# One decoder layer on one core: the moving operand of the feature-major products is read from its last column to its first

## The chip, the cores and the metric

One core of a Trainium2 chip (trn2) runs the whole program. The metric is the device time of one execution in microseconds (us). The profile shows one execution; its span runs from the first to the last instruction of the core.

## What is computed

One hybrid decoder layer for 256 tokens of width 2048, in float32:

```python
proj = x @ w_in                                  # 16 heads of 128: q, k, v
a_out = diff_attention(q_d, k_d, v_d, ...)       # 8 heads, two sub-heads of 64, softmax(1) - lam * softmax(2)
b_out = moba_attention(q_m, k_m, v_m, ...)       # 8 heads, causal (256 tokens are one block)
h = LayerNorm(alpha * x + concat(a_out, b_out) @ w_out)
u = h @ w_up; g, val = u[..., :5632], u[..., 5632:]
gc = conv_b + sum(conv_w[j] * shifted(g, j))     # causal convolution over 3 tokens
out = LayerNorm(alpha * h + (silu(gc) * val) @ w_down)
```

## The kernel before

**Products from halves.** Every float32 operand of the large products is split into a high part rounded to a shorter mantissa and a low part (the remainder), both of the type fp32r. A product is then hi·hi + hi·lo + lo·hi. ACT makes the high part of a weight tile (L138, `split`), DVE the low part (L139); both go two stream steps ahead of the product.

**The stream.** Weights come as 1 MB tiles in one fixed order, `stream`: four groups of four v tiles followed by the q and k tiles of four heads; 16 tiles of the output projection; 43 further pairs of gate and value tiles of the feed-forward part (kinds g and u; the first pair is computed another way, in `mm_first`); 44 tiles of the down projection (kind d). For each tile the loop calls `begin(i)` (splits for later tiles, the next load, work due at this step), the product with `middle(i)` in its middle, and `done(i)`. What is due at a step was registered with `at(step, fn, ...)`. So the order on every engine is written out by hand.

**Feature-major products** (`mm_feature`) are those whose output has features on the partitions and tokens on the columns: q and k of each head (32 tiles) and the gate and value tiles (86). The weights are the stationary operand and the tokens move: `x2` and `h2` are tiles [128, 16, 2, 256] in SBUF, for each of 16 contraction blocks the high parts of the 256 tokens followed by their low parts. For each block one product of 512 columns multiplies the high weights with both, which fills a whole PSUM bank [hi·hi | hi·lo], and a second of 256 columns adds lo·hi to the half that holds hi·hi. Afterwards `added` (L219, L220) takes the bank apart: ACT copies one half to SBUF, DVE adds the other half to it. It is called by `qk_out` for q and k, one step after the product and before the rotation (`rope`, L268 to L271), the scores (two steps after the k tile) and the softmax; by `up_out` for the gate and value tiles, followed by `gated` (L443 to L446) and `act_out` (L450). q and k use banks 0 and 1 in turn; gate and value tiles go around all eight.

Token-major products (v, the output projection, the down projection), the transposes, the scores and the products with probabilities don't use `mm_feature` or `added`. The scores' operands and the probabilities are plain float32, not fp32r. In the profile `bank<-h,hi` is a product that writes a bank, moves the tile h (`h2`) and holds hi (the high weights); `bank<-x,lo` moves `x2` against the low weights. All products share L206.

Of the kernel before, what the change touches and what calls it, by code (L numbers as in the profile page):

```python
# [13 lines left out]
AF = mybir.ActivationFunctionType  # L14
ALU = mybir.AluOpType
# [3 lines left out]
S = 256  # L19
# [5 lines left out]
KT = D // P  # L25
# [25 lines left out]
def hymba_layer(ctx: ExitStack, tc: tile.TileContext, a: dict):  # L51
    nc = tc.nc
    PE, DVE, ACT, POOL, SP = nc.tensor, nc.vector, nc.scalar, nc.gpsimd, nc.sync
# [88 lines left out]
    def weights(i, x, w):  # L142

        hi, lo = parts[i, x // 1024]
        return hi[:, x % 1024:x % 1024 + w], lo[:, x % 1024:x % 1024 + w]
# [59 lines left out]
    def mm(out, lhsT, rhs, start, stop):  # L205
        PE.matmul(out, lhsT, rhs, start=start, stop=stop)  # L206

    def mm_feature(dst, i, t2):

        for k in range(KT):  # L210
            if k == KT // 2:
                middle(i)
            wh, wl = weights(i, k * P, P)
            mm(dst, wh, t2[:, k].rearrange("p j t -> p (j t)"), k == 0, False)
            mm(dst[:, 0:S], wl, t2[:, k, 0], False, k == KT - 1)

    def added(dst, src):

        ACT.activation(dst, src[:, S:2 * S], AF.Copy)  # L219
        DVE.tensor_tensor(dst, src[:, 0:S], dst, ALU.add)  # L220

    def mm_token(dst, i, x, ah, al, first, last):

# [30 lines left out]
    def qk_out(h, j):  # L254
        if j == 0:
            att[h] = work.tile([P, 2, S], F32, name="m1")
        added(att[h][:, j], bank[j])
# [166 lines left out]
    def summed(f, j):  # L424
        t = work.tile([P, S], F32, name="gu"[j] + "s", tag=f"e{j}", bufs=3)
        added(t, u_bank(f, j))
        return t
# [149 lines left out]
    def middle(i):  # L577

        urgent(i + 0.5)
        if i + 2 < NS and seven(i + 2):  # L580
            blocks_lo(i + 2, 0)
            blocks_sum(i + 2, 0)
            blocks_lo(i + 2, 1)
            act_sums_split(i + 2)
            blocks_hi(i + 2, 0)
            split(i + 3, 0)
            blocks_lo(i + 2, 2)
        elif i + 3 < NS and not seven(i + 3):
            split(i + 3, 0)
        pending(i + 0.5)  # L590
# [14 lines left out]
    def run_a(i):  # L605
        kind, h, kc, _ = stream[i]
        if kind == "v":
# [10 lines left out]
            return  # L618
        j = "qk".index(kind)
        mm_feature(bank[j], i, x2)  # L620
        done(i)
        if i < first_o - 1:
# [195 lines left out]
    for i in range(first_u + 2, first_d):  # L818
        begin(i)
        kind, f, _, _ = stream[i]  # L820
        j = "gu".index(kind)
        mm_feature(u_bank(f, j), i, h2)
        done(i)
        if i < first_d - 1:
            at(i + 1, up_out, f, j)
        else:
            up_out(f, j)
        if j == 1 and 3 <= f < 11:
            at(i + 1.5, h_piece, f - 3)
# [90 lines left out]
    for i in range(first_d, NS - PAIRED_END):  # L920
        begin(i)
        _, p, n, _ = stream[i]
# [167 lines left out]
```

## Time and profile before

| | before |
|---|---|
| median of 3 runs | 1138.34 us (1137.75 to 1139.84) |
| the profiled execution | 1139.33 us, of which the span 1137.5 us |
| PE (products) busy | 1124.0 us, 99% |
| PEld (weight loads) busy | 962.2 us, 85% |
| DVE busy | 810.0 us, 71% |
| ACT busy | 614.7 us, 54% |
| mean granted clock of TensorE | 0.997 of full speed |

PE's and PEld's records overlap, and so do the records of neighbouring products: the recorded length of a product includes the time until its last column has left the array, so the distance between the starts of neighbouring products, not their length, is what each costs. Idle time of an engine that isn't the bottleneck costs nothing.

### The profile page before, as it was taken

Reading aid. Unit: us, or ns where it says so; the run is one execution under the profiler, and the core shown is the slowest. Engines: PE = TensorE matmul, PEld = TensorE weight load, DVE = VectorE, ACT = ScalarE, POOL = GpSimd, SP = SyncE. Lnnn points to the kernel's source line nnn. Section 1 sums busy time; section 2 is a strip of 40 time slices with the busy share of each in tenths; the row PEclk is TensorE's granted clock in tenths of the full one; section 3 lists DMA queues with packets and bytes.
Section 4 is the critical chain, followed back from the end, with each engine's and each line's share of the span. In section 5 each row is a group of like instructions: output and inputs, shape, how many; then the busy total and the mean of one; then the engine's idle time right before and its main releaser. Section 6 shows DMA issues by size and latency. Waiting matters only on the chain.

```text
span 1137.5 us, 15607 instructions
## 1 busy us (share of the span) xinstructions
PE 1124.0 (99%) x5971; PEld 962.2 (85%) x5971; DVE 810.0 (71%) x1373; ACT 614.7 (54%) x1007; POOL 30.1 (3%) x38
## 2 busy tenths in 40 slices
PE   9999999999999999999999999999999999999996
PEld 6888888888888898888888888888888888888875
DVE  6895886857745777777566666656666788899885
ACT  6565564444443375545545454555545677667661
POOL 0000000000000000000000000000000000000004
PEclk9999999999999999999999999999999999999998
DMA  9755454545455546555555555555555678777951
GB/s 344 270 222 194 150 185 154 180 172 169 177 185 185 185 173 237 187 197 193 199 185 186 185 186 190 192 199 193 188 186 186 185 232 258 243 218 229 305 189 74
DMA packets 47323, 226.56 MB, mean 199 GB/s; under 512 B 4624, under 2 KB 6544, under 8 KB 27664
## 3 DMA queue, kind: packets, MB, share of 16 engines
q1 hardware_dynamic: 45664, 216.92, 53.8%
q0 software_dynamic: 1584, 8.65, 3.8%
q8 instruction: 46, 0.75, 0.3%
q14 instruction: 29, 0.24, 0.1%
HBM read 214.80 MB, written 2.10 MB: 191 GB/s over the span
## 4 chain that ended last, share of the span: by engine, by line
PE 97%; DMA 1%; DVE 1%; ACT 0%; issue 0%; POOL 0%; SPq 0%; ACTq 0%
PE bank L206 96%; DMA slot<-raw 1%; PE bank L329 0%; DMA raw<-in_w_v 0%; DVE z L977 0%; PE bank L705 0%; PE bank L376 0%; ACT hf L708 0%; ACT slot L516 0%; DVE h L720 0%; DVE st L400 0%; DVE z L397 0%; POOL rstd L408 0%; DVE z L1019 0%; DVE bank L1018 0%
## 5 line engine op out<-in xcount | busy, mean ns | idle before, releaser
L139 DVE TENSOR_TENSOR lo<-raw,hi 128x1024 fp32r<-128x1024 f32 (+1 forms) x372 | 440.6, 1199 | 212.6 <-ACT hi L138 212.4
L138 ACT ACTIVATE hi<-raw 128x1024 fp32r<-128x1024 f32 (+1 forms) x372 | 380.1, 1035 | 229.3 <-PE bank L206 199.6
L206 PE MATMUL bank<-h,hi 128*128 128x512 f32 x1376 | 477.2, 390 | 0.0
L206 PE MATMUL bank<-h,lo 128*128 128x256 f32 x1376 | 388.1, 282 | 0.0
L206 PEld LDWEIGHTS bank<-h,hi 128*128 128x128 f32 x1376 | 258.4, 188 | 53.9
L206 PEld LDWEIGHTS bank<-h,lo 128*128 128x128 f32 x1376 | 260.5, 189 | 0.0
L206 PE MATMUL bank<-x,hi 128*128 128x512 f32 x512 | 181.6, 396 | 0.0
L206 PE MATMUL bank<-x,lo 128*128 128x256 f32 x512 | 144.3, 282 | 0.0
L206 PEld LDWEIGHTS bank<-x,hi 128*128 128x128 f32 x512 | 96.1, 188 | 21.6 <-issue 1.3
L206 PEld LDWEIGHTS bank<-x,lo 128*128 128x128 f32 x512 | 96.9, 189 | 0.2
L206 PE MATMUL bank<-hi,x 128*128 128x512 f32 x256 | 86.6, 408 | 0.6 <-ACT hi L138 0.6
L206 PEld LDWEIGHTS bank<-hi,x 128*128 128x128 f32 x256 | 49.2, 192 | 13.2 <-ACT hi L138 1.5
L443 ACT ACTIVATE gc<-gs,vec 128x256 f32<-128x256 f32 x43 | 25.9, 602 | 58.6 <-DVE gs L220 58.6
L206 PE MATMUL bank<-lo,x 128*128 128x512 f32 x128 | 51.6, 403 | 0.0
L446 ACT ACTIVATE gc<-gc 128x256 f32<-128x256 f32 x44 | 18.4, 418 | 48.9 <-DVE gc L445 48.9
L206 PE MATMUL bank<-hi,mh 128*128 128x512 f32 x128 | 42.1, 400 | 0.0
L206 PE MATMUL bank<-lo,mh 128*128 128x512 f32 x128 | 41.6, 396 | 0.0
L206 PE MATMUL bank<-hi,ml 128*128 128x512 f32 x128 | 41.6, 395 | 0.0
L444 DVE SCALAR_TENSOR_TENSOR gc<-gs,vec,gc 128x255 f32<-128x255 f32 x43 | 20.8, 484 | 28.8 <-ACT gc L443 28.8
L206 PE MATMUL bank<-hi,ah 128*128 128x512 f32 (+1 forms) x126 | 40.3, 395 | 0.0
L206 PE MATMUL bank<-lo,ah 128*128 128x512 f32 (+1 forms) x126 | 39.7, 389 | 0.0
L206 PE MATMUL bank<-hi,al 128*128 128x512 f32 (+1 forms) x126 | 39.6, 389 | 0.0
(176 smaller groups left out, 1284.1 us busy)
## 6 DMA issues: line engine op xcount, KB each, us to landing
raw<-in_w_u SPq DMA_DIRECT2D x88, 1024.0 KB, 4.8
raw<-in_w_d SPq DMA_DIRECT2D x88, 512.0 KB, 6.0
raw<-in_w_qk SPq DMA_DIRECT2D x32, 1024.0 KB, 4.9
raw<-in_w_o SPq DMA_DIRECT2D x16, 1024.0 KB, 4.8
raw<-in_w_v SPq DMA_DIRECT2D x12, 1024.0 KB, 4.8
slot<-raw POOLq DMA_DIRECT2D x11, 768.0 KB, 9.0
raw<-in_w_v SPq DMA_DIRECT2D x8, 256.0 KB, 4.4
raw<-in_w_v SPq DMA_DIRECT2D x4, 512.0 KB, 7.2
```

What stands on the lines that cost most here:

```text
L138: ACT.activation(hi[:, s], t[:, x:y], AF.Copy)
L139: DVE.tensor_tensor(lo[:, s], t[:, x:y], hi[:, s].bitcast(F32), ALU.subtract)
L206: PE.matmul(out, lhsT, rhs, start=start, stop=stop)
L443: ACT.activation(gc, g, AF.Identity, bias=vec[:, C_CB + f:C_CB + f + 1], scale=w[2])
L444: DVE.scalar_tensor_tensor(gc[:, 1:], g[:, 0:S - 1], w[1], gc[:, 1:], op0=ALU.mult, op1=ALU.add)
L446: ACT.activation(gc, gc, AF.Silu)
```

## The change

In `mm_feature` both products read the tokens with a step of -1: column 0 of the bank gets the last low part, column 511 the first high part. hi·hi then lies backwards in columns 256 to 511, and lo·hi is added there, also from tokens read backwards. `added` reads both halves of the bank backwards, so that its output has the tokens in their old order. Nothing else differs: the same number of products, of the same sizes, on the same banks, at the same places of the order, with the weights as before; no transfer is changed.

```diff
             wh, wl = weights(i, k * P, P)
-            mm(dst, wh, t2[:, k].rearrange("p j t -> p (j t)"), k == 0, False)
-            mm(dst[:, 0:S], wl, t2[:, k, 0], False, k == KT - 1)
+            mm(dst, wh, t2[:, k].rearrange("p j t -> p (j t)")[:, ::-1], k == 0, False)
+            mm(dst[:, S:2 * S], wl, t2[:, k, 0, ::-1], False, k == KT - 1)
 
     def added(dst, src):
 
-        ACT.activation(dst, src[:, S:2 * S], AF.Copy)
-        DVE.tensor_tensor(dst, src[:, 0:S], dst, ALU.add)
+        ACT.activation(dst, src[:, 0:S][:, ::-1], AF.Copy)
+        DVE.tensor_tensor(dst, src[:, S:2 * S][:, ::-1], dst, ALU.add)
```

## Rows read from the trace of the kernel before

**Rows 1.** The page: busy time of each engine with its share of the span and its instructions, and the granted clock of TensorE in 40 equal slices of the span (tenths of full speed, 9 is 90% or more).

```profile
PE 1124.0 (99%) x5971; PEld 962.2 (85%) x5971; DVE 810.0 (71%) x1373; ACT 614.7 (54%) x1007; POOL 30.1 (3%) x38
PEclk9999999999999999999999999999999999999998
```

**Rows 2.** All waits of PE: who waited for whom, us in total, times, the longest.

```profile
PE bank L206 <- DVE idle L546: 1.2, 1, 1.2
PE bank L206 <- DVE h L720: 0.7, 1, 0.7
PE bank L206 <- ACT hi L138: 0.6, 1, 0.6
```

**Rows 3.** Groups of instructions by line, operands and shape, the four forms of the feature-major products: count, busy us, mean ns of one, idle time before.

```profile
L206 PE MATMUL bank<-h,hi 128*128 128x512 f32 x1376 | 477.2, 390 | 0.0
L206 PE MATMUL bank<-h,lo 128*128 128x256 f32 x1376 | 388.1, 282 | 0.0
L206 PE MATMUL bank<-x,hi 128*128 128x512 f32 x512 | 181.6, 396 | 0.0
L206 PE MATMUL bank<-x,lo 128*128 128x256 f32 x512 | 144.3, 282 | 0.0
```

**Rows 4.** The instructions of L206, one group: shortest, median and longest duration in ns, and the starts of the first and of the last (us).

```profile
L206 PE MATMUL bank<-h,hi x1376: 389/390/477, 412.0 to 889.1; 128*128 128x512 f32 x197
```

**Rows 5.** Timeline of PE in the gate and value stage (start us, length us): the first three products of a stretch and one product 33 pairs behind the first.

```profile
449.92 0.39 PE L206 MATMUL bank<-h,hi 128*128 128x512 f32 x1
450.14 0.28 PE L206 MATMUL bank<-h,lo 128*128 128x256 f32 x1
450.26 0.39 PE L206 MATMUL bank<-h,hi 128*128 128x512 f32 x1
...
461.36 0.39 PE L206 MATMUL bank<-h,hi 128*128 128x512 f32 x1
```

**Rows 6.** Timeline of PE in the output projection, where products of 512 columns follow each other on two banks in turn; each row is a merged pair.

```profile
330.19 0.63 PE L206 MATMUL bank<-hi,mh 128*128 128x512 f32 x2
...
332.52 0.63 PE L206 MATMUL bank<-hi,ml 128*128 128x512 f32 x2
```

**Rows 7.** Groups by shape: products whose operands are plain float32.

```profile
L206 PE MATMUL bank<-m 128*128 128x256 f32 x16 | 4.8, 381 | 0.0
L206 PE MATMUL bank<-pt,val 128*128 128x256 f32 x16 | 4.8, 379 | 0.0
L206 PE MATMUL bank<-val,pt 128*128 128x128 f32 x48 | 6.6, 275 | 0.0
```

**Rows 8.** Groups by shape: the two instructions of `added`, for value tiles (us), gate tiles (gs) and q and k (m).

```profile
L220 DVE TENSOR_TENSOR us<-bank,us 128x256 f32<-128x256 f32 x43 | 17.9, 417 | 0.0
L220 DVE TENSOR_TENSOR gs<-bank,gs 128x256 f32<-128x256 f32 x43 | 17.9, 417 | 0.0
L219 ACT ACTIVATE gs<-bank 128x256 f32<-128x256 f32 x43 | 15.7, 364 | 0.0
L219 ACT ACTIVATE us<-bank 128x256 f32<-128x256 f32 x43 | 15.5, 360 | 0.0
L220 DVE TENSOR_TENSOR m<-bank,m 128x256 f32<-128x256 f32 x32 | 13.5, 423 | 15.4 <-ACT m L219 15.1
L219 ACT ACTIVATE m<-bank 128x256 f32<-128x256 f32 x32 | 12.3, 383 | 31.3 <-PE bank L206 30.9
```

**Rows 9.** Busy time of each engine in three stretches (the tightest one of DVE; q, k and v; gate and value tiles). Columns: stretch, its length, then busy us and instructions of PE, PEld, DVE, ACT, POOL, the granted clock, the share of the DMA engines and GB/s.

```profile
56.00:75.00 19.00, 19.00 (x122) 16.40 (x121) 16.59 (x42) 11.14 (x30) 1.18 (x2) 1.00 0.67 250
32.00:310.00 278.00, 278.00 (x1555) 238.73 (x1554) 212.82 (x487) 146.90 (x300) 5.54 (x8) 1.00 0.52 183
423.00:892.00 469.00, 469.00 (x2704) 415.75 (x2703) 303.49 (x405) 239.09 (x348) 0.00 (x0) 1.00 0.56 195
```

**Rows 10.** Timeline from the k tile of a head to its scores.

```profile
117.47 0.38 ACT L219 ACTIVATE m<-bank 128x256 f32<-128x256 f32 x1 [1.83 <-PE bank L206]
...
117.89 0.42 DVE L220 TENSOR_TENSOR m<-bank,m 128x256 f32<-128x256 f32 x1 [0.99 <-ACT m L219]
...
119.64 0.43 DVE L271 TENSOR_TENSOR m<-m,sh 128x256 f32<-128x256 f32 x1
...
119.98 2.46 DVE L139 TENSOR_TENSOR lo<-raw,hi 128x1024 fp32r<-128x1024 f32 x2
...
122.91 0.93 PE L206 MATMUL bank<-m 64*128 64x128 f32 x8
```

**Rows 11.** Timeline of one value tile's `added` and the product with the gate behind it.

```profile
502.40 0.36 ACT L219 ACTIVATE us<-bank 128x256 f32<-128x256 f32 x1
...
503.86 0.42 DVE L220 TENSOR_TENSOR us<-bank,us 128x256 f32<-128x256 f32 x1
...
504.31 0.42 DVE L450 TENSOR_TENSOR act<-us,gc 128x256 f32<-128x256 f32 x1
```

**Rows 12.** Groups by shape: the two DVE instructions of the convolution. L444 reads and writes `gc` from its element 1 on, L445 from its element 2 on; both read the gate tile from element 0.

```profile
L444 DVE SCALAR_TENSOR_TENSOR gc<-gs,vec,gc 128x255 f32<-128x255 f32 x43 | 20.8, 484 | 28.8 <-ACT gc L443 28.8
L445 DVE SCALAR_TENSOR_TENSOR gc<-gs,vec,gc 128x254 f32<-128x254 f32 x43 | 20.8, 484 | 1.5
```

## The prediction

> **What bounds the kernel.** I read the busy shares first: PE is busy for 1124.0 of 1137.5 us and its clock stands at the top slot of the row in all slices but the last [rows 1]. A busy PE alone proves little, so the next view is the list of PE's waits: three of them, 2.5 us in all [rows 2]. From there on the order of products is the time, and what a change does is read from the distance between the starts of products. The feature-major ones are 1376 + 512 = 1888 pairs of a 512-column and a 256-column product [rows 3]. From 449.92 to 461.36 us lie 33 pairs, so a pair takes 11.44 / 33 = 346.7 ns; the short product starts some 0.22 us behind the long one, the next long one 0.12 us behind that [rows 5]. Over the whole stage it is the same: 1375 pairs from 412.0 to 889.1 us are 347.0 ns each [rows 4]. So 1888 x 346.7 ns = 655 us, 57% of the span, go through the two edited products. At the 2.4 GHz level one column per cycle makes 768 / 2.4 = 320 ns of a pair; 26.7 ns are something fixed. The engine therefore takes one fp32r column per cycle when it reads forwards, with nothing to spare: any slower reading backwards goes into the time in full.
>
> **The change part by part.** No instruction is added or taken away, no queue or order changes, no transfer moves.
>
> *The moving operand, 1888 times 768 columns.* Nothing in this trace reads a moving operand backwards, so the price is bounded from both sides. Lower end: no cost. The address goes by one element either way, each column is still next to the one before it, and the run is 2 KB long. Upper end: the rows of products that do move slower, those of plain float32. A product of 256 such columns is recorded with 381 and 379 ns [rows 7], one of 256 fp32r columns with 282 ns [rows 3]: 99 ns more for 256 columns, or 0.387 ns per column, nearly a second 2.4 GHz cycle (0.417). If reading backwards cost that, a pair would gain 768 x 0.387 = 297 ns and the kernel 1888 x 297 ns = 561 us. I take the lower end. What the float32 rows show is a type that the array takes in at half rate: from 128 to 256 columns they grow by 379 - 275 = 104 ns [rows 7], 0.81 ns a column. That says that the array can be fed at half rate, not that a step of -1 does it; the operand that changes only its sign of step is nearest to the fp32r rows themselves.
>
> Here the trace can be weighed against the Trainium skill, in sentences that the sum does without. Its page "SBUF — State Buffer" (Door 1: The DMA port swizzle) says that SBUF is read in lines of 16 bytes and that full rate wants at least two hits on a line one after the other: backwards, four float32 columns still share a line, so by that rule the pair stays at 346.7 ns and the sum at no change. Its page "Vector Engine (DVE) Microarchitecture Reference" (5.2 Measured stream behaviour on trn2) speaks against the change: full rate wants runs of neighbouring words that begin on an 8-byte boundary, pairs that begin on an odd word cost 1.30 instead of 1.05 ns a column, and a run read backwards begins on an odd word. In this trace a convolution step that takes one source and its output from an odd element on takes as long as its neighbour from an even one, 484 ns each [rows 12]; that is one odd source, where the page's figure is for both, and it is DVE and not PE.
>
> *Where the sums land.* The 256-column product now adds into columns 256 to 511 instead of 0 to 255. Counted in columns, an element of the shared half was added to 512 columns after the long product wrote it and met the next long product 256 columns later; now it is 256 and then 512. The shortest distance stays 256 columns, so no new wait for an unfinished sum: 0. The weight loads aren't touched: 0.
>
> *The copy in `added`, 32 + 86 times on ACT.* Forwards 383 ns for q and k and 360 to 364 ns for the others [rows 8]. Unknown backwards; bounds: nothing, and double by the same factor of two as above, 32 x 383 + 86 x 362 ns = 43 us of ACT work in all. *The addition, as often on DVE.* 423 and 417 ns; doubled, 32 x 423 + 86 x 417 ns = 49 us. A gain from reading backwards is excluded: the forward rate is already that of neighbouring words. Taken: nothing. Even the upper end lies beside products: over the gate and value tiles DVE would have 303.5 + 35.9 = 339 us of work in 469, ACT 239.1 + 31.1 = 270 [rows 9]. In DVE's tightest stretch, 16.59 of 19 us, at most four additions fall (a tile takes 16 x 346.7 ns = 5.55 us), and 16.59 + 4 x 0.42 = 18.3 still fits [rows 9]. What waits behind them: for q and k, the rotation and then PE's scores. In the row shown the rotation ends at 119.64 + 0.43 = 120.07 us and the scores start at 122.91, 2.84 us later [rows 10]; two doubled instructions eat 0.38 + 0.42 = 0.81 us of it. Behind them on DVE stand two low parts of weights (119.98), made two tiles, 11 us, ahead of their product. For gate and value tiles the output goes into the gate's product on DVE [rows 11] and is needed by PE only in the down projection, after 889 us; their bank comes round again after eight tiles, 44 us. So 0 at both ends, by cover; without any cover for the heads it would be 32 x 0.81 = 26 us.
>
> **Sum.** 0 + 0 + 0 + 0 on the profiled execution: 1139.33 us (span 1137.5 and 1.83 around it). That execution lies 0.99 us, 0.09%, above the median of the three runs, so for a median I say 1138.5 us, its own range 1136 to 1141. The runs before spread over 0.18%, so 0.2% is about what a measurement can tell from no change.
>
> **The rivals.**
>
> *A. PE reads backwards at a lower rate; slower.* Place: every one of the 1888 pairs; it decides as soon as reading takes more than 0.42 ns a column, since nothing covers PE. Price: at the half rate of the float32 rows 1139.3 + 561 = 1700 us; anything between is possible if only some steps (the borders of a memory line, say) cost more: a tenth of that bound, 30 ns a pair, is 56 us and gives 1195 us. For it: PE stands at one column per cycle with no reserve, and no row shows a moving operand with any step but +1. Against it: the neighbouring words are the same words. The 8-byte rule of the skill's vector page would be this rival with a price of its own: 1.30 / 1.05 on the 320 ns of streaming is an estimate of 75 ns a pair, or 142 us, if it held for PE; no row here shows it. Chance 0.18, two thirds of it near the half rate.
>
> *B. The products are unharmed, but the bank is read so much slower that PE waits.* Place: the scores, behind rotation and addition. Point: the two instructions must together grow by more than 2.84 us, to 4.5 times their 0.81 us [rows 8, 10], or push the low parts of weights back by a tile. Price: with half of the heads' 26 us exposed, 1152 us, with all of it 1165. For it: DVE at 87% in the tightest stretch [rows 9]. Against: the slack just named. Chance 0.03.
>
> *C. Faster.* The 26.7 ns fixed per pair could be a pause between a product's last columns and the next one's first in the same bank, which the other order avoids; all of it gone would be 1888 x 26.7 ns = 50 us, so 1089 us. Against: in the output projection, on two banks in turn, ten products of 512 columns start within 332.52 - 330.19 = 2.33 us, 233 ns each [rows 6], 20 ns above 512 / 2.4 = 213; the fixed part stands there too, without a shared bank. Chance 0.03.
>
> **Numbers.** No change 0.76, A 0.18, B 0.03, C 0.03. The no-change case moves out of its 0.2% by chance 2 times in 100 to each side. Same: 0.72. Faster: 0.03 + 0.02 = 0.05. Slower: 0.18 + 0.03 + 0.02 = 0.23. The range starts at 1135, just below the case's own, and goes up to 1165 to take in B and the mildest part of A; 0.76 + 0.03 and some 0.02 of A are inside. It leaves out C's full gain and most of A, about 2 in 10.
>
> **What would show it.** Right: in the changed profile `bank<-h,hi` and `bank<-h,lo` still start 346.7 ns a pair with 390 and 282 ns each, PE's waits stay near 2.5 us, and L219 and L220 keep 360 to 383 and 417 to 423 ns or, if longer, end with the scores still waiting for nothing. Wrong by A: the same products are recorded longer, the 512-column one by up to 198 ns and the 256-column one by up to 99, the gate and value stage stretches from 477 us, and ACT and DVE wait more for PE. Wrong by B: the products as before, but a wait of PE's products or weight loads on L220, L271 or L139. Wrong by C: pairs below 346 ns.

## The result, and the profile after

| | before | changed |
|---|---|---|
| median | 1138.8 us (1137.75 to 1139.84, 4 runs) | 1146.67 us (1146.37 to 1147.63, 4 runs) |
| ratio | | 1.0068, 95% interval 1.0054 to 1.0082 |
| span of the profiled execution | 1137.5 us | 1144.6 us |

The change makes the kernel slower by 7.9 us, 0.68%. No change had been forecast as the likeliest case. The time lies in the stated range, though by a cause for which the range had little room (see below).

First the page's busy times, then all waits of PE in the changed kernel.

```profile
PE 1130.3 (99%) x5971; PEld 957.5 (84%) x5971; DVE 810.1 (71%) x1373; ACT 615.0 (54%) x1007; POOL 30.2 (3%) x38
```

```profile
PE bank L206 <- DVE idle L546: 1.2, 1, 1.2
PE bank L206 <- DVE h L720: 0.7, 1, 0.7
PE bank L206 <- DMA slot<-raw: 0.5, 1, 0.5
PE bank L206 <- ACT hi L138: 0.5, 1, 0.5
PE bank L206 <- DVE lo L139: 0.4, 2, 0.2
```

PE is busy for 6.3 us more than in [rows 1], with the same instructions; DVE and ACT do what they did. PE's waits are 3.3 us instead of 2.5 [rows 2]. So nothing new is being waited for: PE's own products take longer. Which ones, the groups by shape tell.

```profile
L206 PE MATMUL bank<-h,hi 128*128 128x512 f32 x1376 | 483.3, 397 | 0.0
L206 PE MATMUL bank<-h,lo 128*128 128x256 f32 x1376 | 388.0, 282 | 0.0
L206 PE MATMUL bank<-x,hi 128*128 128x512 f32 x512 | 183.8, 402 | 0.0
L206 PE MATMUL bank<-x,lo 128*128 128x256 f32 x512 | 144.4, 282 | 0.0
```

Against [rows 3] the long products are recorded 6 to 7 ns longer, the short ones as before. The distance between starts, which is what counts, is in the timeline: the first products of a stretch and one 36 pairs behind the first.

```profile
449.15 0.40 PE L206 MATMUL bank<-h,hi 128*128 128x512 f32 x1
449.38 0.28 PE L206 MATMUL bank<-h,lo 128*128 128x256 f32 x1
449.50 0.40 PE L206 MATMUL bank<-h,hi 128*128 128x512 f32 x1
...
461.79 0.40 PE L206 MATMUL bank<-h,hi 128*128 128x512 f32 x1
```

12.64 / 36 = 351.1 ns a pair, 4.4 ns more than in [rows 5]; the short product still has a long one 0.12 us behind it, so the added time lies between the start of the long product and that of the short one (0.23 us instead of 0.22). Over the stages, the starts of the first and of the last long product:

```profile
L206 PE MATMUL bank<-h,hi x1376: 397/397/482, 412.5 to 895.8; 128*128 128x512 f32 x197
L206 PE MATMUL bank<-x,hi x512: 395/397/585, 28.7 to 304.0; 128*128 128x512 f32 x171
```

The gate and value stage takes 483.3 us instead of 477.1 [rows 4]: 6.2 us over 1375 pairs, 4.5 ns each. The q and k stage holds 512 more pairs, 512 x 4.5 = 2.3 us. 8.5 us together; the median moved by 7.9, and the span by 7.1, since the first q product of this execution happens to start 1.5 us earlier than in the kernel before (28.7 instead of 30.2 us):

```profile
L206 PE MATMUL bank<-x,hi x512: 389/390/581, 30.2 to 303.4; 128*128 128x512 f32 x171
```

### The profile page after: what moved, and what is told of

It is laid out like the page before. It is cut to its first block, busy times and chain, and to the rows that moved or that the text cites. A ratio compares the mean times of both kernels' runs of the same rounds, so it can differ in the third digit from the quotient of the medians.

```text
span 1144.6 us, 15610 instructions
## 1 busy us (share of the span) xinstructions
PE 1130.3 (99%) x5971; PEld 957.5 (84%) x5971; DVE 810.1 (71%) x1373; ACT 615.0 (54%) x1007; POOL 30.2 (3%) x38
## 4 chain that ended last, share of the span: by engine, by line
PE 97%; DMA 1%; DVE 1%; ACT 0%; issue 0%; SPq 0%; POOL 0%; ACTq 0%
PE bank L206 96%; DMA slot<-raw 1%; PE bank L329 0%; DMA raw<-in_w_v 0%; DVE z L977 0%; PE bank L705 0%; PE bank L376 0%; ACT hf L708 0%; ACT slot L516 0%; DVE h L720 0%; DVE st L400 0%; DVE z L397 0%; POOL rstd L408 0%; DVE z L1019 0%; SPq L155 0%
## 5 line engine op out<-in xcount | busy, mean ns | idle before, releaser
L139 DVE TENSOR_TENSOR lo<-raw,hi 128x1024 fp32r<-128x1024 f32 (+1 forms) x372 | 440.8, 1200 | 219.3 <-ACT hi L138 218.4
L206 PE MATMUL bank<-h,hi 128*128 128x512 f32 x1376 | 483.3, 397 | 0.0
L206 PE MATMUL bank<-h,lo 128*128 128x256 f32 x1376 | 388.0, 282 | 0.0
L206 PEld LDWEIGHTS bank<-h,hi 128*128 128x128 f32 x1376 | 258.7, 188 | 62.3
L206 PEld LDWEIGHTS bank<-h,lo 128*128 128x128 f32 x1376 | 258.7, 188 | 0.0
L206 PE MATMUL bank<-x,hi 128*128 128x512 f32 x512 | 183.8, 402 | 0.0
L206 PE MATMUL bank<-x,lo 128*128 128x256 f32 x512 | 144.4, 282 | 0.0
L206 PEld LDWEIGHTS bank<-x,hi 128*128 128x128 f32 x512 | 96.3, 188 | 24.3 <-issue 1.3
L206 PEld LDWEIGHTS bank<-x,lo 128*128 128x128 f32 x512 | 96.3, 188 | 0.2
L206 PE MATMUL bank<-hi,x 128*128 128x512 f32 x256 | 84.9, 402 | 0.5 <-ACT hi L138 0.5
L206 PEld LDWEIGHTS bank<-hi,x 128*128 128x128 f32 x256 | 48.1, 188 | 12.8 <-ACT hi L138 1.4
L206 PE MATMUL bank<-lo,x 128*128 128x512 f32 x128 | 50.8, 397 | 0.4 <-DVE lo L139 0.4
L206 PE MATMUL bank<-hi,mh 128*128 128x512 f32 x128 | 42.1, 399 | 0.0
L206 PE MATMUL bank<-hi,ml 128*128 128x512 f32 x128 | 41.6, 395 | 0.0
L206 PE MATMUL bank<-lo,mh 128*128 128x512 f32 x128 | 41.6, 395 | 0.0
L444 DVE SCALAR_TENSOR_TENSOR gc<-gs,vec,gc 128x255 f32<-128x255 f32 x43 | 20.8, 484 | 28.8 <-ACT gc L443 28.8
L206 PE MATMUL bank<-hi,ah 128*128 128x512 f32 (+1 forms) x126 | 40.2, 394 | 0.0
L206 PE MATMUL bank<-lo,ah 128*128 128x512 f32 (+1 forms) x126 | 39.7, 389 | 0.0
L206 PE MATMUL bank<-hi,al 128*128 128x512 f32 (+1 forms) x126 | 39.6, 389 | 0.0
```

Of the source, the lines that this page charges most:

```text
L139: DVE.tensor_tensor(lo[:, s], t[:, x:y], hi[:, s].bitcast(F32), ALU.subtract)
L444: DVE.scalar_tensor_tensor(gc[:, 1:], g[:, 0:S - 1], w[1], gc[:, 1:], op0=ALU.mult, op1=ALU.add)
```

## Experiments

Two theories stood at the start. *Direction*: reading the tokens backwards costs 4.5 ns per long product. *Placement*: the sum that the short product adds to now lies in the half of the bank that the long product wrote last, and that costs it. The measure below is the number of us from the first to the last long product of the gate and value stage, divided by its 1375 distances; it holds one break at the start of the stage, so it reads 347.0 for the kernel before, where a stretch inside the stage reads 346.7. Placement, direction and halves were executed several times; every other kernel below ran once, so that its total is one execution. The granted clock was 0.996 or 0.997 in all of them. Where single distances are given to the ns, they are differences of the starts that the trace records.

### Placement alone, direction alone

```diff
-    xh, xl = x2[:, :, 0], x2[:, :, 1]          # the same for hh, hl and h2
+    xl, xh = x2[:, :, 0], x2[:, :, 1]
...
             mm(dst, wh, t2[:, k].rearrange("p j t -> p (j t)"), k == 0, False)
-            mm(dst[:, 0:S], wl, t2[:, k, 0], False, k == KT - 1)
+            mm(dst[:, S:2 * S], wl, t2[:, k, 1], False, k == KT - 1)
...                                            # added: the two halves change places too
```

> Placement alone: the low parts lie ahead of the high parts in x2 and h2, so that read forwards the bank holds [hi.lo | hi.hi] and the short product adds into columns 256 to 511, as in the changed kernel, but nothing is read backwards. Theory 1 (direction: a descending read of the 512 columns costs some 4.5 ns more): the long product's length stays 390 ns, a pair 346.7 ns, the gate and value stage 477 us, the time that of the kernel before, 1139 us. Theory 2 (placement: the sum added into the half that was written last costs it): 397 ns, 351.2 ns a pair, 483 us, 1146.7 us, as in the changed kernel.

With the same swap of the tiles, but both products read backwards:

```diff
+            mm(dst, wh, t2[:, k].rearrange("p j t -> p (j t)")[:, ::-1], k == 0, False)
+            mm(dst[:, 0:S], wl, t2[:, k, 1, ::-1], False, k == KT - 1)
...                                            # added: the two halves change places too
```

> Direction alone: low parts ahead of high parts in the tiles and both products read backwards, so that the bank holds [hi.hi | hi.lo] with the tokens reversed and the short product adds into columns 0 to 255, as in the kernel before; the two halves are read backwards in the addition. Theory 1 (direction): long product 397 ns, 351.2 ns a pair, 483 us for the gate and value stage, 1146.7 us. Theory 2 (placement): 390 ns, 346.7 ns, 477 us, 1139 us. If direction and placement each carry a part, both this and the run of placement alone lie between.

The instructions of L206, placement alone, then direction alone (shortest, median and longest ns; first and last start):

```profile
L206 PE MATMUL bank<-h,hi x1376: 390/390/477, 411.4 to 888.5; 128*128 128x512 f32 x197
```

```profile
L206 PE MATMUL bank<-h,hi x1376: 397/397/482, 412.5 to 895.7; 128*128 128x512 f32 x197
```

Placement alone: 477.1 us, median 1139.11 us against 1139.04 of the kernel before, ratio 1.0002 (0.9993 to 1.0011). Direction alone: 483.2 us, median 1147.65 us, ratio 1.0073 (1.006 to 1.0085). The placement theory is out: the whole cost is the direction's.

### Which of the two products

The changed kernel with the short product forwards again, and the changed kernel with the long one forwards:

```diff
-            mm(dst[:, S:2 * S], wl, t2[:, k, 0, ::-1], False, k == KT - 1)
+            mm(dst[:, S:2 * S], wl, t2[:, k, 0], False, k == KT - 1)
```

> The changed kernel with the short product (256 columns) read forwards again; it adds the tokens of lo.hi in the wrong order, so that this part of the sums is not the layer's. Theory 1, if the long read alone carries the cost: 351.2 ns a pair as in the changed kernel, long to short 233 ns, short to long 118 ns. If the short read carries part of it, less than that.

```diff
-            mm(dst, wh, t2[:, k].rearrange("p j t -> p (j t)")[:, ::-1], k == 0, False)
+            mm(dst, wh, t2[:, k].rearrange("p j t -> p (j t)"), k == 0, False)
```

> The changed kernel with the long product (512 columns) read forwards and the short one backwards; the halves then come in the wrong order, so that the sums of the q, k, gate and value tiles are not the layer's. Theory 1, if the long read alone carries the cost: 346.7 ns a pair, the gate and value stage 477 us, the time that of the kernel before. If the short descending read costs something that shows, up to 351 ns.

The rows of long only, then of short only:

```profile
L206 PE MATMUL bank<-h,hi x1376: 394/397/481, 413.9 to 900.2; 128*128 128x512 f32 x197
```

```profile
L206 PE MATMUL bank<-h,hi x1376: 391/394/476, 411.6 to 888.7; 128*128 128x512 f32 x197
L206 PE MATMUL bank<-h,lo x1376: 278/279/286, 411.8 to 889.0; 128*128 128x256 f32 x197
```

Only the short one backwards costs nothing: 477.1 us, one execution of 1139.39 us. Its records only shift 3 to 4 ns from the short product to the long one. Only the long one backwards costs more than both: 486.3 us, 353.7 ns a pair, 1151.02 us. That was not expected, since 351 had been said. So the long product carries the cost. That the forward neighbour adds the other 2 ns doesn't follow: in the last experiment below a kernel with both products backwards stands at the same level.

### Where the run begins

The long product forwards but one word further on, so that it begins on an odd word; and backwards one word further on, so that it begins on an even one.

```diff
+            f = t2.rearrange("p k j t -> p (k j t)")
+            o = 2 * S * k + (1 if k < KT - 1 else -1)
+            mm(dst, wh, f[:, o:o + 2 * S], k == 0, False)              # second kernel: [:, ::-1]
```

> The kernel before, its 512-column product read forwards but from one word further on (from element 1 of a contraction block into the first element of the next, and for the last block one word earlier), so that the run begins on an odd word; the tokens of that product are displaced by one, so that the sums of the feature-major products are not the layer's. Theory S (a run that begins on an odd word is what costs, the descending run does so): 351 ns a pair, the gate and value stage 483 us, about 1147 us. Theory D (the descending direction costs): 346.7 ns, 477 us, 1139 us.

> The changed kernel, its 512-column product read backwards from one word further on, so that the descending run begins on an even word, the first of its line; the tokens of that product are displaced by one, so that the sums of the feature-major products are not the layer's. Theory S (the odd word costs): 346.7 ns a pair, 477 us for the gate and value stage, 1139 us. Theory D (the direction costs): 351.2 ns, 483 us, 1147 us, or more if the run now also touches one line more.

```profile
L206 PE MATMUL bank<-h,hi x1376: 390/397/472, 413.6 to 899.2; 128*128 128x512 f32 x197
```

```profile
L206 PE MATMUL bank<-h,hi x1376: 394/394/478, 415.0 to 901.9; 128*128 128x512 f32 x197
```

Forwards from one word further on: 485.6 us, 353.2 ns a pair, 1149.83 us. A displacement by one word can thus cost PE 6 ns per long product without any reversal. But a begin on an odd word is not enough for that. The last block of each tile begins one word earlier, on an odd word as well, and its long product is the middle one here, recorded as short as in the kernel before:

```profile
503.62 0.40 PE L206 MATMUL bank<-h,hi 128*128 128x512 f32 x1
...
503.97 0.39 PE L206 MATMUL bank<-h,hi 128*128 128x512 f32 x1
...
504.32 0.40 PE L206 MATMUL bank<-h,hi 128*128 128x512 f32 x1
```

From the start of such a last block's product to that of the next long one it is 346 to 348 ns in 84 of 85 cases of the stage; for the other blocks, the break at the start of the stage left out, it is 352 to 355 ns in 1282 of 1288. And in the q and k stage the same displaced reading goes at either price. These are the long products of two windows, 126 to 129.5 and 188.5 to 193.5 us:

```profile
L206 PE MATMUL bank<-x,hi x12: 390/390/392, 125.6 to 129.4; 128*128 128x512 f32 x12
L206 PE MATMUL bank<-x,hi x15: 397/397/398, 188.2 to 193.2; 128*128 128x512 f32 x15
```

Of 448 such pairs in that stage, 138 take at most 348 ns, no more than an undisplaced one; they come in stretches behind a pause between products. So the price of the displaced run isn't a matter of its addresses alone, and what sets it stays open. The descending runs do without such free stretches: no pair of the changed kernel, outside a pause, takes less than 350 ns.

Backwards from an even word: 486.9 us, 354.1 ns, 1152.13 us, no cheaper. The begin on an odd word is not the explanation of the descending run's cost.

### Fewer columns

The long product cut to 384 columns, forwards and backwards; the addition, and in the backward kernel the short product's place in the bank, follow (not shown).

```diff
+            mm(dst[:, 0:384], wh, t2[:, k].rearrange("p j t -> p (j t)")[:, 0:384], k == 0, False)   # second kernel: [:, ::-1]
```

> The kernel before with the long product cut to its first 384 columns (the low parts of the last 128 tokens left out, and the addition takes columns 128 to 383 for its second half, so that the sums are not the layer's). It is the measure for the next kernel: 128 columns less at the 2.4 GHz level, 53.3 ns, so 346.7 - 53.3 = 293.4 ns a pair.

> The same 384 columns and the short product read backwards (the same part of the sums left out). The difference to the forward one, pair by pair. If a descending long product costs a fixed amount: 4.5 ns more, 297.9 ns. If it costs by the column: 4.5 x 384 / 512 = 3.4 ns more, 296.8 ns. If only what goes beyond the 256 columns of the short product, which showed no cost, counts: 4.5 x 128 / 256 = 2.2 ns more, 295.6 ns.

```profile
L206 PE MATMUL bank<-h,hi x1376: 331/337/420, 385.4 to 790.7; 128*128 128x384 f32 x197
```

```profile
L206 PE MATMUL bank<-h,hi x1376: 338/340/422, 386.5 to 793.4; 128*128 128x384 f32 x197
```

405.3 and 406.9 us: 294.8 and 295.9 ns a pair; one execution each, 1041.34 and 1043.81 us. But these stages are no clean measure. Both kernels have four pauses of PE between 470 and 503 us, which the kernel before hasn't: PE waits for low parts of weights (L139). One of them, in the forward kernel:

```profile
480.21 0.34 PE L206 MATMUL bank<-h,hi 128*128 128x384 f32 x1
481.20 0.38 PE L206 MATMUL bank<-h,lo 128*128 128x256 f32 x1 [0.65 <-DVE lo L139]
```

Behind them, in the window from 510 to 785 us, forwards and then backwards:

```profile
L206 PE MATMUL bank<-h,hi x944: 333/336/339, 509.8 to 784.8; 128*128 128x384 f32 x189
L206 PE MATMUL bank<-h,hi x939: 340/340/341, 509.8 to 784.9; 128*128 128x384 f32 x188
```

275.0 us over 943 distances are 291.6 ns a pair, 275.1 over 938 are 293.3: 1.7 ns apart. None of the three sizes that had been worked out fits; the smallest, 2.2 ns, is the nearest. The forward kernel itself lies 1.8 ns below the 293.4 that 128 columns less should give. A fixed 4.5 ns per long product is excluded; more doesn't follow.

### Which order it is: of lines, of words, of halves

Each half of the tokens backwards, but the halves in order (`t2[:, k, :, ::-1]`, sums in columns 0 to 255); groups of four words in descending order with the words inside ascending; and the reverse of this. In the second and third the addition puts the tokens back in the same way; dst4 is the bank in the same groups.

```diff
+            mm(dst.rearrange("p (j t) -> p j t", t=S), wh, t2[:, k, :, ::-1], k == 0, False)          # halves
+            mm(dst4, wh, t2[:, k].rearrange("p j t -> p (j t)").rearrange("p (a b) -> p a b", b=4)[:, ::-1, :], ...)   # groups
+            mm(dst4, wh, t2[:, k].rearrange("p j t -> p (j t)").rearrange("p (a b) -> p a b", b=4)[:, :, ::-1], ...)   # words
```

> The tokens run backwards inside each half, but the halves keep their order: the long product reads two descending runs of 256 columns, the short one a descending run of 256 columns; the short product adds into columns 0 to 255. Theory R (a descending run costs only for what goes beyond 256 columns, or where it passes from one half of the tile into the other): 346.7 ns a pair, 477 us from the first to the last long product of the gate and value stage, 1139 us. Theory D (every descending long product costs, however it is cut): 351.2 ns or more, 483 us, 1147 us.

> Groups of four words (16 bytes) in descending order, the words inside a group in ascending order, in both products and in the addition. If the order of the groups is what costs: 351 ns a pair, 483 us, 1147 us. If the order inside a group is what costs: 346.7 ns, 477 us, 1139 us. If a pattern of short runs costs something by itself, both this and the next one lie above 351 ns.

> The complement: groups of four words in ascending order, the words inside a group in descending order, in both products and in the addition. If the order of the groups costs: 346.7 ns a pair, 477 us, 1139 us. If the order inside a group, or the odd word that the first run begins on, costs: 351 ns or more, 483 us, 1147 us.

Halves, groups, words:

```profile
L206 PE MATMUL bank<-h,hi x1376: 397/397/482, 413.7 to 897.0; 128*128 128x512 f32 x197
```

```profile
L206 PE MATMUL bank<-h,hi x1376: 396/397/482, 413.1 to 896.3; 128*128 128x512 f32 x197
```

```profile
L206 PE MATMUL bank<-h,hi x1376: 389/391/477, 411.5 to 888.6; 128*128 128x512 f32 x197
```

Halves: 483.3 us, median 1146.63 us, ratio 1.0066 (1.0049 to 1.0082): it is not the step over the middle, nor a run longer than 256 columns. Groups descending: 483.2 us, 1147.09 us, the whole cost, although the words inside ascend and the run begins on an even word. Words descending inside ascending groups: 477.1 us, 1139.17 us, no cost, although every word is read in an order turned around and the run begins on an odd word. So what costs is the order in which 16-byte groups come, and inside such a group the order is free.

### Eight tiles of each reading in one execution

> Several readings of the tokens in one execution, eight of the 86 gate and value tiles each (128 pairs), each with product lines of its own; the halves aren't put back in order, and two readings use only 64 of the 128 weight columns, so that the sums of these tiles are not the layer's. Forwards (control): 346.7 ns a pair; backwards as in the changed kernel (control): 351.2. Groups of 8, of 16 and of 64 words in descending order, the words inside in ascending order: if a descending step between lines of 16 bytes costs each time, the 4.5 ns shrink as the steps do, to about 2.3, 1.1 and 0.3 ns; if what counts is a larger unit, they stay at 4.5 ns up to the size of this unit and vanish beyond it. Forwards from word 2, word 4 and word 16 of the block instead of word 0: if the begin inside a line of 16 bytes is what cost 6 ns a pair with the odd word, word 2 costs about as much and words 4 and 16 nothing; if the unit is larger, word 4 costs too. 64 weight columns, forwards and backwards (the load of the weights is then half as long): if the descending read is slow by itself, the backward pairs are 4.5 ns longer than the forward ones, or up to 6.8 if the short product's part had been covered by the weight load; if it collides with the reading of the weights, the difference shrinks towards half or nothing.

One edit of the kind for each reading, as `elif n == 4: PE.matmul(grouped(dst, 64), wh, grouped(both, 64)[:, ::-1], ...)`, where n counts blocks of eight tiles. Each reading has a line of its own; in order: backwards; groups of 8, of 16 and of 64 words descending; 64 weight columns forwards and backwards; forwards from word 2, 4 and 16; and last the control, the lines left as they were, in the window behind the readings.

```profile
L227 PE MATMUL bank<-h,hi x128: 395/398/400, 456.4 to 501.3; 128*128 128x512 f32 x128
L230 PE MATMUL bank<-h,hi x128: 394/395/396, 501.7 to 546.2; 128*128 128x512 f32 x128
L233 PE MATMUL bank<-h,hi x128: 394/398/403, 546.6 to 591.5; 128*128 128x512 f32 x128
L236 PE MATMUL bank<-h,hi x128: 390/390/394, 591.8 to 635.8; 128*128 128x512 f32 x128
L239 PEld LDWEIGHTS bank<-h,hi x128: 133/135/139, 636.1 to 680.1; 128*64 128x64 f32 x128
L239 PE MATMUL bank<-h,hi x128: 391/392/400, 636.2 to 680.2; 128*64 128x512 f32 x128
L242 PE MATMUL bank<-h,hi x128: 396/397/398, 680.6 to 725.5; 128*64 128x512 f32 x128
L245 PE MATMUL bank<-h,hi x128: 389/390/400, 725.8 to 769.9; 128*128 128x512 f32 x128
L248 PE MATMUL bank<-h,hi x128: 387/391/398, 770.3 to 814.4; 128*128 128x512 f32 x128
L251 PE MATMUL bank<-h,hi x128: 389/393/398, 814.8 to 858.9; 128*128 128x512 f32 x128
L254 PE MATMUL bank<-h,hi x96: 390/390/397, 859.2 to 892.2; 128*128 128x512 f32 x96
```

127 distances each, 95 for the control. The starts are printed here to 0.1 us; the pairs below are worked out from the timeline, which gives them to 0.01 us. Control 346.8 ns; backwards 353.3; groups of 8 words 351.1; of 16 words 353.3; of 64 words 346.7, no cost left. The cost doesn't shrink with the number of descending steps and vanishes between groups of 64 and of 256 bytes: a larger unit than the 16-byte group counts, as the second possibility had it. The backwards control, the same products as in the changed kernel, stands here at 353.3 instead of 351.1: the price has two levels, some 4.5 and some 6.6 ns, and which of them holds isn't a matter of the reading alone. Single distances show that the levels are averages over a rhythm: here 352 and 355 ns in turn, in the groups of 16 words 351 and 356, in the changed kernel's gate and value stage 350, 351 and 352. After some pauses of its q and k stage (one lies at 55 us) the changed kernel goes in the rhythm of 352 and 355 too. So a level belongs to a stretch of the execution; what sets the rhythm stays open.

64 weight columns: forwards 346.8 ns, backwards 353.3. The weight loads are recorded at 135 ns instead of 188, and the difference between the directions is still that of the controls. A collision with the weights' reading, which should shrink with their load, is not supported. Nor does the length of the load set the pair: with half the weights it takes as long.

Forwards from word 2, 4 or 16: 347.4 to 347.5 ns, within 1 ns of word 0. None of them costs what the begin at word 1 costs in most of its stretches.

## Why the prediction was right and wrong, step by step

- *What bounds the kernel*: right. PE stays the chain, without a new wait of weight; a few ns per product went into the time in full, as said of rival A.
- *The moving operand*: the step that failed. The term was taken at its lower end, 0, with the reason that the operand that changes only its sign of step is nearest to the fp32r rows. It measured 4.5 ns a pair, 1.5% of the 297 ns that the upper end allowed; 1888 x 4.5 = 8.5 us, where the median moved by 7.9. The two ends were right, the choice between them was not: "nearest" was argued for a rate per column, and what came is a few ns per long product (384 columns pay 1.7 ns, 256 nothing).
- *The range* (1135 to 1165 us) holds the measured 1146.67 us by luck: its upper part had been set for rival B, which didn't occur, and for the mildest part of A, given 0.02. The mildest price that A works out from rows is 56 us, outside the range.
- *Rival A* is the case that came, at about a seventh of the mild price that had been worked out (56 us). Its remark that only some steps might cost more, those at the borders of a memory line, points the right way, though the price doesn't go by the number of the steps. Its point of decision, more than 0.42 ns a column, was not the one.
- *The weighing of the Trainium skill's pages.* The Trainium skill's page "SBUF — State Buffer" (Door 1: The DMA port swizzle) gives lines of 16 bytes and full rate from two hits on a line. The runs agree that inside 16 bytes the order is free (347.0 ns a pair over the stage, as before); they differ where groups descend, which costs 4.5 ns a pair although each still gets its four hits. The rule of the Trainium skill's page "Vector Engine (DVE) Microarchitecture Reference" (5.2 Measured stream behaviour on trn2), runs that begin on an 8-byte boundary, isn't borne out on PE: an ascending run from word 1 costs 6 ns a pair in most stretches but nothing in others, the last blocks, which begin on an odd word too, pay nothing, and neither do descending words inside ascending groups. The price that the prediction estimated from its ratio of 1.30 to 1.05 (75 ns a pair; the working gives 76) doesn't carry over, and the descending run's cost isn't explained by it.
- *Where the sums land*: right, 0. Placement alone has a ratio of 1.0002.
- *The copy and the addition*: right, nothing. The rows that answer to [rows 8]:

```profile
L220 DVE TENSOR_TENSOR us<-bank,us 128x256 f32<-128x256 f32 x43 | 18.0, 418 | 0.0
L219 ACT ACTIVATE gs<-bank 128x256 f32<-128x256 f32 x43 | 15.7, 366 | 0.0
L219 ACT ACTIVATE us<-bank 128x256 f32<-128x256 f32 x43 | 15.6, 364 | 0.0
```

  Read backwards from PSUM, DVE takes 418 instead of 417 ns and ACT 364 to 366 instead of 360 to 364, so the cover that was worked out wasn't needed, and rival B fell with it.
- *Rival C*: excluded; the fixed 26.7 ns of a pair only grew.
- *What would show it*: the 390 ns of the long product were the right row to watch, and by their 397 the change shows at a glance; but "slower" had been tied to growth in both products, and only the long one grew.

What stays open: why descending groups of up to 64 bytes cost a long product 4.5 to 6.6 ns and a 256-column one nothing; what sets the rhythm behind its two levels, and lets a run displaced by one word go free in some stretches; and what in the engine the unit between 64 and 256 bytes is. A fetch ahead in ascending order would fit the groups of 64 words, but it is only argued: no run here separates it from a unit of the memory.

## What to carry to other kernels

Where PE is the chain, an edit that leaves every instruction in place can still cost: compare the recorded length of the products and the distance of their starts, and multiply a few ns by their number. Where an operand has to be read backwards, do it inside 16-byte groups or in steps of 256-byte blocks, or turn it around where it is drained: DVE and ACT read 256 columns of PSUM backwards at the forward price. Don't displace a moving operand by one word: forwards from word 1 cost 6 ns a pair in most stretches, from words 2, 4 and 16 less than 1. And measure such prices inside a stretch without pauses, over several stretches: the same products stood at two levels in one kernel.

## What the runs showed of the hardware that was not expected

- An fp32r product of 512 columns whose moving operand is read in descending 16-byte groups starts the next one 4.5 to 6.6 ns later (351.1 to 353.5 ns a pair against 346.7); with 64-word groups, or descending words inside 16 bytes, it doesn't.
- A moving operand read in ascending order from word 1 of its block costs 6 ns per product of 512 columns in most stretches (353.2 against 347.0 ns a pair over the stage) and nothing in others (138 of 448 pairs of the q and k stage), nor where it begins one word early, on an odd word too; from words 2, 4 and 16 it is less than 1 ns.
- A 256-column product read backwards costs nothing between the starts (477.1 us for the stage), and halving the weight columns (loads of 135 instead of 188 ns) leaves the pair at 346.8 ns.
